# RWKV's triangular inverses on four quarters of the TensorE array, and a fourth raw weight buffer from the FFN on

## The chip, the cores and the metric

The kernel runs on one core of a Trainium2 chip. The metric is device microseconds (us) of one launch. The kernel before has a median of 892.22 us over three runs (888.31 to 893.76).

## The reference, cut to what matters

Two blocks of a language model run one after the other on 256 tokens of width 1024, in fp32. The first block mixes with RWKV-7 and with retention, merges both through gates, and follows with a convolved FFN (width 2816); the second has a Mamba-2 mixer, a per-layer embedding, sliding-window attention and another embedding. The change touches the inside of RWKV-7 and the loading of weights.

RWKV-7's delta rule is computed in chunks of 64 tokens. For each of 8 heads and each of 4 chunks a 64x64 unit lower triangular matrix must be inverted: 32 inverses.

```python
def first_block(x, positions, ...):
    ...
        y_rw = rwkv7_mixer(p_rw, ...)
        y_ret = retention_mixer(p_ret, positions)
        merged = (jax.nn.sigmoid(g_rw.astype(jnp.float32)) * (y_rw @ w_branch_rw[l])
                  + jax.nn.sigmoid(g_ret.astype(jnp.float32)) * (y_ret @ w_branch_ret[l]))
        h = h + rms_norm(merged @ w_out[l], norm_mix_post[l])
        f = conv_ffn(rms_norm(h, norm_ffn_pre[l]), ffn_w_up[l], ffn_conv_w[l], ffn_conv_b[l], ffn_w_down[l])
        h = h + rms_norm(f, norm_ffn_post[l])
```

## The kernel before, in words

**Weights.** Every large matmul takes its weights from a `Stream` (lines 214 to 247). `next()` takes a raw buffer of 128x1024 fp32 (512 KB) and has SyncE's queue load it (L232). ScalarE rounds it to the high part (`whi`, `lhi`, ... L254) and VectorE subtracts that from the raw values for the low part (L255); L249 and L250 are the same with a gain. A product is three matmuls, high times high, high times low, low times high (L258 to L260). `raw_turn` (L211) names the raw buffers, three of them, taken in turn; a load waits until ScalarE and VectorE are done with what its buffer held. In the last stages a second pool of three is added.

**Inverses.** `product` (L600) makes eight 64x64 fp32 matmuls (L606) into one PSUM bank: four pairs of heads `f`, and for each the two heads `x`. Head x=0 has its rows in partitions 64 to 127, head x=1 in 0 to 63, and each writes the partitions that it reads, so two of the array's four 64x64 quarters work, those on its diagonal. The trace shows two MATMUL records for each of these fp32 matmuls. `inverse(c)` (L611) inverts the eight matrices of chunk c by doubling the size of the blocks in five rounds. A round is a product of the matrix with the transposed estimate `Tm`, a copy of it to SBUF with its sign turned (`Pn`, ScalarE, L621), a product of the estimate `X` with that, a masked copy into `Tm` (VectorE, L626) and a transpose of `Tm` into `X` (VectorE, L627). The last round has no transpose (L630).

**Order.** `rwkv` (L636) runs the inverses of four chunks in step, a half round at a time; after them it walks through the chunks: a right-hand side (L650, L653), a copy `R` (L655), a product with the inverse (L606), copies into `VU` (L658, L659), a new state (L666). Outputs follow for each two chunks (L690, L696), then normalisation, transposes (L716) and gating. `weave` puts a step of this between steps of the other stream: the projections of retention and of the gates, whose large matmuls fill TensorE while RWKV's small steps wait for ScalarE and VectorE. The framework then orders each engine's instructions; each engine works through its own in that order.

**Pools.** `cst` holds all constants, `msk` the masks of the inverses, both for the whole program. Pool `p1` lives through the mixers, and `late_pool` opens after it.

## Time and profile before

| | |
|---|---|
| profiled execution | 891.34 us |
| its span | 889.5 us |
| median of 3 runs | 892.22 us |
| TensorE busy (PE) | 858.5 us, 97% of the span |
| VectorE busy (DVE) | 651.4 us, 73% |
| ScalarE busy (ACT) | 522.6 us, 59% |
| share of 16 DMA engines in SyncE's loads | 48.0% |

PE is TensorE's matmul row, PEld its weight loads, SP is SyncE, whose queue issues the loads. A row of the timeline merges instructions of one group that follow each other: start, time from the first start to the last end, engine, line, and in brackets the idle time of the engine just before and what ended it. In groups, "x16 | 6.3, 421 | 0.1" says sixteen instructions, 6.3 us busy, 421 ns each on average, 0.1 us of idle time before them. Instructions of one engine overlap at their ends, so a mean is longer than the step from one to the next.

### The profile page before, as it was taken

Reading aid. Unit: us, or ns where it says so; the run is one execution under the profiler, and the core shown is the slowest. Engines: PE = TensorE matmul, PEld = TensorE weight load, DVE = VectorE, ACT = ScalarE, POOL = GpSimd, SP = SyncE. Lnnn points to the kernel's source line nnn. Section 1 sums busy time; section 2 is a strip of 40 time slices with the busy share of each in tenths; the row PEclk is TensorE's granted clock in tenths of the full one; section 3 lists DMA queues with packets and bytes.
Section 4 is the critical chain, followed back from the end, with each engine's and each line's share of the span. In section 5 each row is a group of like instructions: output and inputs, shape, how many; then the busy total and the mean of one; then the engine's idle time right before and its main releaser. Section 6 shows DMA issues by size and latency. Waiting matters only on the chain.

```text
span 889.5 us, 15883 instructions
## 1 busy us (share of the span) xinstructions
PE 858.5 (97%) x6226; PEld 749.9 (84%) x6226; DVE 651.4 (73%) x1117; ACT 522.6 (59%) x935; POOL 70.6 (8%) x105
## 2 busy tenths in 40 slices
PE   9999999999999999999999988999999999999997
PEld 6788788789998889989999878988888888878776
DVE  7778865774755778888788878889775569857643
ACT  6555533454544556656656657768776467756652
POOL 2000000100100100000000000001101003402000
PEclk9999999999999999999999999999999999999999
DMA  8443341334566476656555376643534558543311
GB/s 278 145 132 105 131 126 68 103 112 137 179 219 213 156 245 212 217 190 188 191 190 178 104 242 209 222 152 141 189 121 141 165 176 289 165 172 105 117 36 36
DMA packets 42284, 144.44 MB, mean 162 GB/s; under 512 B 5009, under 2 KB 5601, under 8 KB 42210
## 3 DMA queue, kind: packets, MB, share of 16 engines
q1 hardware_dynamic: 41600, 141.32, 48.0%
q0 software_dynamic: 608, 2.11, 0.9%
q8 instruction: 49, 0.80, 0.4%
q14 instruction: 25, 0.20, 0.1%
q10 hardware_dynamic: 2, 0.00, 0.0%
HBM read 140.24 MB, written 3.18 MB: 161 GB/s over the span
## 4 chain that ended last, share of the span: by engine, by line
PE 44%; issue 23%; DVE 14%; DMA 9%; ACT 5%; POOL 3%; ACTq 0%; POOLq 0%; SPq 0%; DVEq 0%
PE mm L258 10%; PE mm L260 10%; PE mm L259 10%; DVE wlo L255 3%; PE sm L606 3%; DMA raw<-in_w_up 3%; DMA raw<-in_w_br 2%; DMA raw<-in_w_down 2%; ACT whi L254 1%; PE sm L260 1%; PE sm L258 1%; PE sm L259 1%; DVE llo L255 1%; PE sm L285 1%; PE sm L1559 1%
## 5 line engine op out<-in xcount | busy, mean ns | idle before, releaser
L254 ACT ACTIVATE whi<-raw 128x1024 fp32r<-128x1024 f32 (+1 forms) x125 | 128.1, 1028 | 111.0 <-PE mm L259 35.2
L255 DVE TENSOR_TENSOR wlo<-raw,whi 128x1024 fp32r<-128x1024 f32 (+1 forms) x124 | 147.2, 1191 | 58.8 <-ACT whi L254 57.4
L260 PE MATMUL mm<-xTh,wlo 128*128 128x256 f32 x616 | 173.7, 282 | 2.8 <-DVE wlo L255 2.8
L258 PE MATMUL mm<-xTh,whi 128*128 128x256 f32 x616 | 174.9, 284 | 0.2 <-ACT xTh L254 0.2
L259 PE MATMUL mm<-xTl,whi 128*128 128x256 f32 x616 | 173.4, 282 | 0.3 <-DVE xTl L255 0.3
L260 PEld LDWEIGHTS mm<-xTh,wlo 128*128 128x128 f32 x616 | 116.2, 189 | 3.9 <-DVE wlo L255 3.5
L258 PEld LDWEIGHTS mm<-xTh,whi 128*128 128x128 f32 x616 | 116.3, 189 | 2.6 <-issue 0.7
L259 PEld LDWEIGHTS mm<-xTl,whi 128*128 128x128 f32 x616 | 116.4, 189 | 2.1 <-DVE xTl L255 0.5
L258 PE MATMUL mm<-whi,xTh 128*128 128x512 f32 x168 | 68.3, 407 | 0.0
L260 PE MATMUL mm<-whi,xTl 128*128 128x512 f32 x168 | 67.3, 401 | 0.0
L259 PE MATMUL mm<-wlo,xTh 128*128 128x512 f32 x168 | 66.0, 394 | 0.0
L258 PE MATMUL mm<-lhi,xTh 128*128 128x512 f32 (+1 forms) x156 | 61.1, 393 | 0.5 <-ACT xTh L254 0.5
L260 PE MATMUL mm<-lhi,xTl 128*128 128x512 f32 (+1 forms) x156 | 60.1, 386 | 0.5 <-DVE xTl L255 0.5
L259 PE MATMUL mm<-llo,xTh 128*128 128x512 f32 (+1 forms) x156 | 60.3, 386 | 0.0
L255 DVE TENSOR_TENSOR llo<-raw,lhi 128x1024 fp32r<-128x1024 f32 x38 | 47.0, 1239 | 11.8 <-ACT lhi L254 11.7
L254 ACT ACTIVATE lhi<-raw 128x1024 fp32r<-128x1024 f32 x38 | 40.0, 1057 | 19.2 <-DMA raw<-in_w_down 12.8
L1010 DVE SCALAR_TENSOR_TENSOR fc<-mm,par,fc 128x255 f32<-128x255 f32 x88 | 42.1, 478 | 8.9 <-ACT fc L1007 8.2
L259 PE MATMUL mm<-xTl,ehi 128*128 128x256 f32 x168 | 47.3, 281 | 0.0
L260 PE MATMUL mm<-xTh,elo 128*128 128x256 f32 x168 | 47.3, 281 | 0.0
L258 PE MATMUL mm<-xTh,ehi 128*128 128x256 f32 x168 | 47.2, 281 | 0.0
L1007 ACT ACTIVATE fc<-mm,par 128x256 f32<-128x256 f32 x44 | 24.4, 554 | 23.8 <-DVE fc L1010 23.8
L255 DVE TENSOR_TENSOR elo<-raw,ehi 128x1024 fp32r<-128x1024 f32 (+1 forms) x27 | 31.8, 1183 | 8.6 <-ACT ehi L254 8.2
(485 smaller groups left out, 2029.3 us busy)
## 6 DMA issues: line engine op xcount, KB each, us to landing
raw<-in_w_up SPq DMA_DIRECT2D x44, 512.0 KB, 4.0
raw<-in_w_xbc SPq DMA_DIRECT2D x25, 512.0 KB, 4.2
raw<-in_w_ret SPq DMA_DIRECT2D x24, 512.0 KB, 3.9
raw<-in_w_down SPq DMA_DIRECT2D x22, 512.0 KB, 4.4
raw<-in_w_gate SPq DMA_DIRECT2D x16, 512.0 KB, 3.6
raw<-in_w_z SPq DMA_DIRECT2D x16, 512.0 KB, 4.0
raw<-in_w_so SPq DMA_DIRECT2D x16, 512.0 KB, 3.8
raw<-in_w_pg SPq DMA_DIRECT2D x16, 512.0 KB, 4.5
```

What stands on the lines that cost most here:

```text
L254: first = S.activation(out=hi, in_=src, func=AF.Copy)
L255: last_split[:] = first.ins, (eng or V).tensor_tensor(out=lo, in0=src, in1=hi.bitcast(F32), op=sub).ins
L258: PE.matmul(out, sh, mh, start=start, stop=False)
L259: PE.matmul(out, sh, ml, start=False, stop=False)
L260: return PE.matmul(out, sl, mh, start=False, stop=stop).ins
L285: last = PE.transpose(ps[:, i, :], src[:, (j + i) * P:(j + i + 1) * P], ident)
L606: PE.matmul(fv(px)[u, f, :], lhsT(f, x), rhs[u, f, :], start=True, stop=True)
L1007: S.activation(out=c, in_=ps, func=AF.Identity, scale=wv[:, (ntap - 1) * nf + i:(ntap - 1) * nf + i + 1], bias=bv[:, i:i + 1])
L1010: V.scalar_tensor_tensor(out=c[:, d:], in0=ps[:, :T - d], scalar=wv[:, j:j + 1], in1=c[:, d:], op0=mult, op1=add)
L1559: PE.matmul(po[:, o:o + 64], eT[:, j * P:(j + 1) * P], vn[kb][:, kv * 64:(kv + 1) * 64], start=(kb == 0), stop=(kb == nk - 1))
```

## The change

Two chunks are now inverted together, by `inverse(p)` for a pair p of chunks. The sixteen heads-by-chunks are dealt to four quarters: s says whether heads 0 to 3 or 4 to 7, x the head as before, k counts the four matrices of one quarter. `product` takes two banks, one for each s, and its loop visits four different quarters one after the other. For s=1 the first product writes the other half of the partitions than it reads (`home`), and the estimate `X` of s=1 lies in that other half, so it is transposed by two instructions of 64 partitions (L637) where s=0 needs one (L634). The walk through the chunks deals its matmuls in the same way and splits `R` and `VU` by s.

The constants are split: those that only the mixers use (`cst1`) and the masks go into pool `p1`. In the room that this frees, `late_pool` holds a fourth raw buffer, `rawl`, which from the FFN on takes its turn after the three others; in the last stages there are seven where there were six. The tables of angles share a `u` buffer.

```diff
 CONST, N_CONST = _layout([
-    ("ident", 128), ("ones2", 128), ("heads2", 2), ("gmask", 128), ("tri", 128), ("amask", 256),
-    ("fdec", 8), ("qdec", 8), ("qd2", 8), ("rdec", 4), ("scan64", 256), ("scan128", 256),
+    ("ident", 128), ("amask", 256), ("scan128", 256),
+    ("ones2", 128), ("heads2", 2), ("gmask", 128), ("tri", 128),
+    ("fdec", 8), ("qdec", 8), ("qd2", 8), ("rdec", 4), ("scan64", 256),
     ("ifreq", 32), ("xinit", 64), ("eye64", 64),
 ])
+N_ALL = CONST["ones2"][0]
...
-    nc.sync.dma_start(out=cst[:, P:], in_=io["cst"][:, P:])
+    nc.sync.dma_start(out=cst1, in_=io["cst"][:, N_ALL:])
+    nc.sync.dma_start(out=cst[:, P:], in_=io["cst"][:, P:N_ALL])
...
-    def product(lhsT, rhs):
-        px = sm()
-        for f in range(4):
+    def home(s, x):
+        return UH[x] if s == 0 else VH[x]
+
+    def product(lhsT, rhs, out):
+        banks = [fv(sm()), fv(sm())]
+        for k in range(4):
+            for s in range(2):
+                for x in range(2):
+                    PE.matmul(banks[s][out(s, x), k, :], lhsT(s, x, k), rhs(s, x, k), start=True, stop=True)
+        return banks
...
-    def inverse(c):
+    def inverse(p):
...
+        def turned(s):
+            if s == 0:
+                V.transpose(out=X[s], in_=Tm[s])
+            else:
+                for x in range(2):
+                    V.transpose(out=X[s][VH[x]], in_=Tm[s][UH[x]])
...
         for i in range(1, 6):
-            pp = product(lambda f, x: Gm[UH[x], c, 2 * f + x, 0:64], Tm)
-            Pn = tl(p1, [P, 4, 64], "Pn", 3)
-            S.activation(out=Pn, in_=pp, func=AF.Copy, scale=-1.0)
+            pp = product(lambda s, x, k: Gm[UH[x], 2 * p + k // 2, 4 * s + 2 * (k % 2) + x, 0:64],
+                         lambda s, x, k: Tm[s][UH[x], k, :], home)
+            Pn = []
+            for s in range(2):
+                Pn.append(tl(p1, [P, 4, 64], "Pn", 4))
+                S.activation(out=Pn[s], in_=pp[s], func=AF.Copy, scale=-1.0)
             yield
             if i < 5:
-                pq = product(lambda f, x: X[UH[x], f, :], Pn)
-                V.copy_predicated(out=Tm, mask=half4(f"m{i}", msk, MASKI), data=pq)
-                V.transpose(out=X, in_=Tm)
+                pq = product(lambda s, x, k: X[s][home(s, x), k, :], lambda s, x, k: Pn[s][home(s, x), k, :],
+                             lambda s, x: UH[x])
+                for s in range(2):
+                    V.copy_predicated(out=Tm[s], mask=mask(f"m{i}"), data=pq[s])
+                    turned(s)
...
-        gens = [inverse(c) for c in range(4)]
+        gens = [inverse(p) for p in range(2)]
...
-            pr = sm()
+            pr = [fv(sm()), fv(sm())]
             R = tl(p1, [P, 4, 64], "R", 1)
-            S.activation(out=R, in_=fv(pr), func=AF.Copy)
+            places = [(f, s, x) for f in range(2) for s in range(2) for x in range(2)]
...
+            for s in range(2):
+                S.activation(out=R[:, 2 * s:2 * s + 2, :], in_=pr[s][:, 0:2, :], func=AF.Copy)
             yield
-            pu = product(lambda f, x: X_c[c][UH[x], f, :], R)
+            pu = [fv(sm()), fv(sm())]
+            for f, s, x in places:
+                PE.matmul(pu[s][UH[x], f, :], X_c[c // 2][s][home(s, x), 2 * (c % 2) + f, :], R[home(s, x), 2 * s + f, :],
+                          start=True, stop=True)
...
     late_pool = pool("late")
     wtags["l"] = (late_pool, 4)
+    raw_turn[:] = [(wp, "raw", 3)] * 3 + [(late_pool, "rawl", 1)]
...
-    raw_turn.append((p4, "raw4", 3))
+    raw_turn[:] = [(wp, "raw", 3), (p4, "raw4", 3)] * 3 + [(late_pool, "rawl", 1)]
```

On TensorE, between the second product of the first round (`sm<-Pn,u`) and the first product of the second (`sm<-u,Gm`), there stood in the kernel before six large matmuls of retention:

```order
L606 MATMUL sm_1339<-Pn_1298,u_1284 64x64 x8
L258 MATMUL mm_1060<-whi_1352,xTh_79 128x512
L259 MATMUL mm_1060<-wlo_1353,xTh_79 128x512
L260 MATMUL mm_1060<-whi_1352,xTl_80 128x512
L258 MATMUL mm_1060<-whi_1352,xTh_79 128x512
L259 MATMUL mm_1060<-wlo_1353,xTh_79 128x512
L260 MATMUL mm_1060<-whi_1352,xTl_80 128x512
L606 MATMUL sm_1362<-u_1236,Gm_262 64x64 x8
```

In the changed kernel the same place reads so; `sm_1330` and `sm_1331` are the banks of s=0 and s=1 of the second pair of chunks, `sm_1365` and `sm_1366` those of the first pair in the next round:

```order
L619 MATMUL sm_1331<-Pn_1299,u_1272 64x64 x2
L619 MATMUL sm_1330<-Pn_1297,u_1267 64x64 x2
L619 MATMUL sm_1331<-Pn_1299,u_1272 64x64 x2
L619 MATMUL sm_1365<-u_1233,Gm_259 64x64 x2
L619 MATMUL sm_1366<-u_1238,Gm_259 64x64 x2
```

Two matmuls of a bank now alternate with two of the other, where eight of one bank stood together, and no large matmul is left between the two products at this one place; at the other changes of product 6 to 12 large ones, or retention's smaller ones, stand between them as before.

On VectorE, the masked copies and transposes after the second product of the first round, up to the next low part of a weight (`wlo`), were in the kernel before:

```order
L255 TENSOR_TENSOR wlo<-raw,whi 128x1024 x2
L626 COPY_PREDICATED u<-msk,sm 128x256 x2
L627 STREAM_TRANSPOSE u<-u 128x256 x2
L626 COPY_PREDICATED u<-msk,sm 128x256 x2
L627 STREAM_TRANSPOSE u<-u 128x256 x2
L255 TENSOR_TENSOR wlo<-raw,whi 128x1024
```

In the changed kernel, with the last two transposes of the setting up (L637) ahead of them:

```order
L256 TENSOR_TENSOR wlo<-raw,whi 128x1024
L637 STREAM_TRANSPOSE u<-u 64x256 x2
L663 COPY_PREDICATED u<-msk,sm 128x256 x2
L634 STREAM_TRANSPOSE u<-u 128x256
L637 STREAM_TRANSPOSE u<-u 64x256 x2
L663 COPY_PREDICATED u<-msk,sm 128x256 x2
L634 STREAM_TRANSPOSE u<-u 128x256
L637 STREAM_TRANSPOSE u<-u 64x256 x2
L256 TENSOR_TENSOR wlo<-raw,whi 128x1024
```

Eight instructions of a round have become ten.

On SyncE's queue in the middle of the FFN, the loads of the up and down weights were in the kernel before:

```order
L232 DMA raw<-in_w_down 128x1024
L232 DMA raw<-in_w_up 128x1024 x2
L232 DMA raw<-in_w_down 128x1024
L232 DMA raw<-in_w_up 128x1024 x2
L232 DMA raw<-in_w_down 128x1024
```

In the changed kernel every fourth goes to `rawl`:

```order
L233 DMA raw<-in_w_down 128x1024
L233 DMA rawl<-in_w_up 128x1024
L233 DMA raw<-in_w_up 128x1024 x3
L233 DMA rawl<-in_w_down 128x1024
L233 DMA raw<-in_w_up 128x1024
L233 DMA rawl<-in_w_up 128x1024
```

A load can now be issued one buffer earlier, and the three of a step of the FFN no longer always stand in the order down, up, up.

## Rows read from the trace of the kernel before

**Rows 1.** Page, busy time of each engine and chain that ended last.

```profile
PE 858.5 (97%) x6226; PEld 749.9 (84%) x6226; DVE 651.4 (73%) x1117; ACT 522.6 (59%) x935; POOL 70.6 (8%) x105
...
PE 44%; issue 23%; DVE 14%; DMA 9%; ACT 5%; POOL 3%; ACTq 0%; POOLq 0%; SPq 0%; DVEq 0%
```

**Rows 2.** Stretches: length, busy PE, PEld, DVE, ACT, POOL, granted clock, DMA share, GB/s.

```profile
109.00:115.78 6.78, 6.78 (x140) 5.62 (x139) 6.23 (x12) 2.68 (x6) 0.00 (x0) 1.00 0.42 131
115.78:149.00 33.22, 33.22 (x616) 28.44 (x615) 19.05 (x40) 13.16 (x25) 0.00 (x0) 1.00 0.32 103
...
325.00:500.00 175.00, 172.67 (x1219) 160.48 (x1218) 144.40 (x239) 109.28 (x177) 0.00 (x0) 1.00 0.58 186
```

**Rows 3.** Timeline of TensorE, products of the inverses on two quarters.

```profile
111.71 0.68 PE L606 MATMUL sm<-u,Gm 64*64 64x64 f32 x16
...
115.78 2.08 PE L606 MATMUL sm<-u,Gm 64*64 64x64 f32 x64
117.79 0.50 PE L258 MATMUL mm<-whi,xTh 128*128 128x512 f32 x1
118.13 0.40 PE L259 MATMUL mm<-wlo,xTh 128*128 128x512 f32 x1
118.36 0.39 PE L260 MATMUL mm<-whi,xTl 128*128 128x512 f32 x1
```

**Rows 4.** Timeline of TensorE, outputs of the last two chunks.

```profile
218.24 0.69 PE L690 MATMUL sm<-St,KR 64*64 64x64 f32 x32
```

**Rows 5.** Groups of VectorE, 109 to 149 us.

```profile
L255 DVE TENSOR_TENSOR wlo<-raw,whi 128x1024 fp32r<-128x1024 f32 x8 | 9.7, 1214 | 6.6 <-ACT whi L254 6.6
L627 DVE STREAM_TRANSPOSE u<-u 128x256 f32<-128x256 f32 x16 | 6.3, 421 | 0.1
L626 DVE COPY_PREDICATED u<-msk,sm 128x256 f32<-128x256 uint8 x16 | 6.2, 425 | 6.5 <-PE sm L606 6.5
```

**Rows 6.** Timeline of VectorE, one round, and its next wait.

```profile
114.05 0.77 DVE L626 COPY_PREDICATED u<-msk,sm 128x256 f32<-128x256 uint8 x2
114.71 0.76 DVE L627 STREAM_TRANSPOSE u<-u 128x256 f32<-128x256 f32 x2
115.40 0.74 DVE L626 COPY_PREDICATED u<-msk,sm 128x256 f32<-128x256 uint8 x2
116.04 0.75 DVE L627 STREAM_TRANSPOSE u<-u 128x256 f32<-128x256 f32 x2
121.06 1.22 DVE L255 TENSOR_TENSOR wlo<-raw,whi 128x1024 fp32r<-128x1024 f32 x1 [4.27 <-ACT whi L254]
```

**Rows 7.** Groups of the walk through the chunks, 149 to 225 us.

```profile
L653 PE MATMUL sm<-VU,Gm 64*64 64x64 f32 x64 | 3.6, 220 | 0.0
L650 PE MATMUL sm<-St,KR 64*64 64x64 f32 x48 | 3.1, 224 | 0.0
...
L606 PE MATMUL sm<-R,u 64*64 64x64 f32 x64 | 2.7, 224 | 0.0
```

**Rows 8.** Timeline of TensorE, transposes that it waited for.

```profile
30.87 0.44 PE L476 MATMUL sm<-cst,u 128*128 128x128 f32 x2 [0.62 <-ACT u L469]
...
190.94 0.63 PE L716 MATMUL sm<-cst,u 128*128 128x128 f32 x4 [0.79 <-DVE u L712]
```

**Rows 9.** Waits, 325 to 500 us (the FFN): total, times, longest.

```profile
ACT lhi L254 <- DMA raw<-in_w_down: 12.8, 13, 1.8
...
ACT ehi L254 <- DMA raw<-in_w_up: 8.3, 5, 2.4
ACT whi L254 <- DMA raw<-in_w_up: 7.4, 7, 1.9
```

**Rows 10.** Timeline in the FFN, ScalarE and TensorE.

```profile
383.25 1.06 ACT L254 ACTIVATE lhi<-raw 128x1024 fp32r<-128x1024 f32 x1 [1.75 <-DMA raw<-in_w_down]
...
385.61 0.50 PE L258 MATMUL sm<-lhi,fah 128*128 128x512 f32 x1 [1.14 <-ACT fah L254]
...
387.09 0.50 PE L260 MATMUL sm<-lhi,fal 128*128 128x512 f32 x1 [0.75 <-DVE fal L255]
```

**Rows 11.** Timeline of TensorE in the Mamba projections.

```profile
543.62 0.38 PE L260 MATMUL mm<-xTh,wlo 128*128 128x256 f32 x1 [1.77 <-DVE wlo L255]
547.98 0.39 PE L260 MATMUL mm<-xTh,wlo 128*128 128x256 f32 x1 [1.03 <-DVE wlo L255]
```

More of the change, by code (lines that the diff above doesn't have):

```diff
@@ L166, in tile_block @@
     ppd = tl(dp, [4, P, D], "ppd")
-    cst = tl(gp, [P, N_CONST], "cst")
+    cst = tl(gp, [P, N_ALL], "cst")
     h_t = [tl(gp, [P, D], f"h{t}") for t in range(2)]
-    msk = tl(gp, [P, N_MASKI], "msk", dt=U8)
     par = tl(gp, [P, N_PAR], "par")
@@ L176, in C @@
         lo, hi = CONST[name]
-        return cst[:, lo:hi]
+        return cst[:, lo:hi] if hi <= N_ALL else cst1[:, lo - N_ALL:hi - N_ALL]
     def PR(name):
@@ L192, in angles @@
     def angles():
-        posf = tl(p1, [P, 4], "posf")
+        room = u2()
+        ang, n, r = (room[:, i * 128:(i + 1) * 128].rearrange("p (a l) -> p a l", a=4) for i in range(3))
+        posf = room[:, 384:388]
         with tc.issue_after(last_split[1]):
             V.tensor_copy(out=posf, in_=pos)
-        ang = tl(p1, [P, 4, 32], "ang")
         V.tensor_tensor(out=ang, in0=posf.unsqueeze(2).to_broadcast([P, 4, 32]),
@@ L326, in tile_block @@
     p1 = pool("p1", ph)
+    cst1 = tl(p1, [P, N_CONST - N_ALL], "cst1")
+    msk = tl(p1, [P, N_MASKI], "msk", dt=U8)
     def u2(shape=(P, 512)):
@@ L595, in fv, with half4 @@
         return ps[:, 0:256].rearrange("p (f l) -> p f l", f=4)
-    def half4(name, const=cst, off=CONST):
-        lo, hi = off[name]
-        return const[:, lo:hi].unsqueeze(1).to_broadcast([P, 4, 64])
-    def product(lhsT, rhs):
-        px = sm()
-        for f in range(4):
-            for x in range(2):
-                u = UH[x]
-                PE.matmul(fv(px)[u, f, :], lhsT(f, x), rhs[u, f, :], start=True, stop=True)
-        return fv(px)
-    X_c = {}
-    def inverse(c):
-        X, Tm = (a_.rearrange("p (f l) -> p f l", f=4) for a_ in duo())
-        for x in range(2):
-            V.tensor_tensor(out=X[UH[x]], in0=Gm[UH[x], c, x::2, 0:64], in1=half4("xinit")[UH[x]], op=mult)
-        V.tensor_tensor(out=X, in0=X, in1=half4("eye64"), op=add)
-        V.transpose(out=Tm, in_=X)
-        for i in range(1, 6):
-            pp = product(lambda f, x: Gm[UH[x], c, 2 * f + x, 0:64], Tm)
-            Pn = tl(p1, [P, 4, 64], "Pn", 3)
-            S.activation(out=Pn, in_=pp, func=AF.Copy, scale=-1.0)
+    def half4(v):
+        return v.unsqueeze(1).to_broadcast([P, 4, 64])
@@ new lines, in mask, with L @@
+    def mask(name):
+        lo, hi = MASKI[name]
+        return half4(msk[:, lo:hi])
+    def home(s, x):
[7 more added lines that the diff above has]
+        return banks
+    X_c = {}
+    def inverse(p):
+        X, Tm = [], []
+        def L(s, x):
+            return Gm[UH[x], 2 * p:2 * p + 2, 4 * s + x:4 * s + 4:2, 0:64]
+        def turned(s):
[4 more added lines that the diff above has]
+                    V.transpose(out=X[s][VH[x]], in_=Tm[s][UH[x]])
+        xinit = C("xinit").unsqueeze(1).unsqueeze(1).to_broadcast([P, 2, 2, 64])
+        for s in range(2):
+            a, b = (a_.rearrange("p (f l) -> p f l", f=4) for a_ in duo())
+            for x in range(2):
+                V.tensor_tensor(out=a[UH[x]].rearrange("p (c f) l -> p c f l", c=2), in0=L(s, x), in1=xinit[UH[x]], op=mult)
+            V.tensor_tensor(out=a, in0=a, in1=half4(C("eye64")), op=add)
+            V.transpose(out=b, in_=a)
+            X.append(a)
+            Tm.append(b)
+            if s:
+                turned(s)
+        for i in range(1, 6):
+            pp = product(lambda s, x, k: Gm[UH[x], 2 * p + k // 2, 4 * s + 2 * (k % 2) + x, 0:64],
[4 more added lines that the diff above has]
+                S.activation(out=Pn[s], in_=pp[s], func=AF.Copy, scale=-1.0)
@@ L622, in inverse @@
             yield
             if i < 5:
-                pq = product(lambda f, x: X[UH[x], f, :], Pn)
-                V.copy_predicated(out=Tm, mask=half4(f"m{i}", msk, MASKI), data=pq)
-                V.transpose(out=X, in_=Tm)
-            else:
-                px = product(lambda f, x: Pn[UH[x], f, :], X)
-                V.copy_predicated(out=X, mask=half4("t5", msk, MASKI), data=px)
+                pq = product(lambda s, x, k: X[s][home(s, x), k, :], lambda s, x, k: Pn[s][home(s, x), k, :],
+                             lambda s, x: UH[x])
@@ L631, in inverse @@
+                for s in range(2):
+                    V.copy_predicated(out=Tm[s], mask=mask(f"m{i}"), data=pq[s])
+                    turned(s)
+            else:
+                px = product(lambda s, x, k: Pn[s][home(s, x), k, :], lambda s, x, k: X[s][home(s, x), k, :], home)
+                for s in range(2):
+                    V.copy_predicated(out=X[s], mask=mask("t5"), data=px[s])
             yield
-        X_c[c] = X
+        X_c[p] = X
     yrT = (tl(p1, [P, 4, T], "yrTh", 1, F32R), tl(p1, [P, 4, T], "yrTl", 1, F32R))
```

26 lines of the change are left out of this document (14 added, 12 removed).

## The prediction

> **What bounds the kernel now.** I read the page's busy times first: TensorE is busy for 858.5 of 889.5 us, VectorE for 73%, and TensorE leads the chain that ended last with 44% [rows 1]. So a change gains where it shortens TensorE's own work or fills one of the 31 us in which it idles. The stretches come next. From 109 to 149 us, where the inverses lie, TensorE has no idle time at all and runs at a granted clock of 1.00, the level of 2.4 GHz; VectorE is busy for 6.23 + 19.05 = 25.3 of these 40 us, ScalarE for 15.8 [rows 2]. In the FFN TensorE idles for only 175 - 172.67 = 2.3 us, with the DMA engines at a share of 0.58 [rows 2]. The timelines then tell what a product of the inverses costs, and the waits what the loads hold up.
>
> **Four quarters.** A half round of the inverses is 64 records of 64x64 on TensorE and takes 2.08 us; 16 records take 0.68 us [rows 3]. The difference, 1.40 us for 48 records, is 29.2 ns each, and 0.21 us is fixed. There the records use two quarters. The outputs of the last two chunks are the one place where the kernel already visits four quarters in turn: x picks the half of the rows, the chunk's parity the half of the columns. Its 32 records take 0.69 us [rows 4], with the same 0.21 us 15.0 ns each, half of 29.2. So four quarters run at once. A half round would take 0.21 + 64 x 0.015 = 1.17 us, 0.91 less.
>
> There are ten half rounds. In the first one, half of the 64 records still run two by two, because the scheduler took the banks of the second pair apart (24 matmuls, later 8): that one saves some 0.5 us. Together 9 x 0.91 + 0.5 = 8.7 us of TensorE time.
>
> Two rules of the Trainium skill speak against this. The 32 records took 0.69 us from the first start to the last end, and one takes 0.22 us; that leaves 15 ns from start to start [rows 4, 7]. The Trainium skill, "TensorE: Matmul & The Clock Gate" (Back-to-back issue gap), gives an issue floor of about 25 ns; by that the 816 records of the change (640 here, 176 in the walk below) would save an estimated 3.4 us instead of 11.2, and the time would be about 888. The row contradicts it for matmuls in different quarters.
>
> The old product writes one bank from both halves of the rows, and its two quarters overlap, with 29.2 ns a record [rows 3]; the row with four at once has one half of the rows to a bank [rows 4]. The Trainium skill, "TensorEngine Tiling (Array Packing)" (Restrictions and Gotchas), says that different row tiles can't use one PSUM bank at the same time. By that rule the new product, which writes each bank from both halves of the rows, would gain nothing; the old one's overlap speaks against it. As a mechanism it is the second rival below.
>
> **What VectorE puts against it.** A round has eight instructions of VectorE on the path from the second product to the next round: 0.77 + 0.76 + 0.74 + 0.75 us less overlaps, from 114.05 to 116.79, 2.74 us [rows 6], or 0.34 us each. It gets ten, 3.4 us: for each pair of chunks two masked copies, then three transposes, of which two have half the partitions. The rows show no transpose of 64 partitions. By rows 5 one of 128 partitions has a mean of 421 ns; I take the same, since each of them still walks through 256 columns, with half of it as the lower bound. Twelve more in all (eight in the rounds, four in the setting up) are 4.1 us at 0.34, 2 at least. VectorE has 40 - 25.3 = 14.7 us free here, and after the change 40 - 7 - 25.3 - 4.1 = 3.6. It still fits, but tightly.
>
> Where does TensorE wait? The next round's first product for a pair needs that pair's two copies. After the second product of the first pair (0.5 us), its copies end some 0.9 us later, the second pair's 1.7 us after them, as three transposes and two copies stand between. Where 12 large matmuls lie between the products, 12 x 0.23 = 2.8 us by the starts of rows 3, both fit beside them. After the first round none lies there, as the order shows: TensorE has one pair's product (0.5 us) as cover each time, and waits about 0.4 + 1.2 = 1.6 us. The last two transposes of the setting up stand behind low parts of weights of 1.2 us each [rows 5], so the second pair's product is late by 0 to 1.5 us, I take 0.6. Before the last round only retention's short matmuls give cover: 0.3. Sum of new waits 2.5 us; bounds 0, and 7.9 if each of the four returns waits like the first and the setting up costs its 1.5. Queued behind a waiting product are retention's large matmuls, and behind those ScalarE's next high part, which waits for the weight buffers.
>
> The inverses give -8.7 + 2.5 = -6.2 us, between -8.7 and -0.8.
>
> **The walk through the chunks.** L653, L650 and L606 have 64 + 48 + 64 = 176 records [rows 7], all on two quarters now and on four after: 176 x 14.2 ns = -2.5 us. The copies R and VU become two of half the size: four more instructions of VectorE, eight of ScalarE, each under the 0.41 and 0.39 us of a whole one. After each of them the order on TensorE puts 4 to 48 large matmuls or retention's, so I cost them at 0.3 us. That is -2.2 us, between -2.5 and 0 (without that cover, 12 times 0.2).
>
> Two waits of TensorE lose their ground by the new order: L716 at 190.94 (0.79 us) gets, by the order, 45 large matmuls ahead of it instead of 38, and L476 at 30.87 (0.62) 19 instead of 8 [rows 8]. I take -1.0, between -1.4 and 0, the work moved being done at another time.
>
> **The fourth raw buffer.** In the FFN ScalarE waits for loads often: 12.8 + 8.3 + 7.4 us [rows 9]. But TensorE's whole idle time there is 2.3 us, and one event makes most of it: the high part of a down weight waits 1.75 us for its load, what ScalarE does next (`fah`) is late, and TensorE waits 1.14 and then 0.75 us [rows 10]. A load issued one buffer earlier ends this. What is late next is VectorE's queue, which costs TensorE nothing there now. I take -1.9; the bound is -2.3, and 0 if the scheduler's other order makes such an event elsewhere. The Mamba projections lose 1.77 + 1.03 us to VectorE [rows 11], whose order between two low parts stays nearly as long: 0, at best -2.8. The seventh buffer of the last stages: 0, within 1 either way. The constants now come in two loads of the same bytes: 0.
>
> **The sum**, against the profiled execution's 891.3 us: -6.2 - 2.2 - 1.0 - 1.9 = -11.3, so 880.0. The median of the runs shown is 0.9 us above the profiled one: 880.9 us. I forecast 881.
>
> **The rivals.**
> - More than that: VectorE keeps up, the new waits come to 0.5 us, and the other order of the Mamba stage lifts its 2.8 us: -2.0 - 2.8 - 1 = 6 us further, 875. For it: VectorE's copies of 64 partitions may be short. Against: VectorE's free time of 3.6 us.
> - The pairs stay pairs: two quarters at a time, whatever the loop. Then the 11.2 us of TensorE time stay, VectorE's extra work hides beside it, and the raw buffer with the two waits gives -2.9: 889. What overlaps in part lies between that and the forecast. Against: rows 4. For: there the banks are dealt in another way.
> - Slower than before: VectorE's and ScalarE's queues, in order, expose each round. Low parts of weights stand ahead of the masked copies, and they wait for ScalarE's high parts, and those for TensorE to free a weight buffer (4.27 us at 121.06) [rows 6]. If the matmul that frees it stands behind the product, the large matmuls cover nothing, and each of four returns shows its 3.4 us, the setting up its 1.5, the walk 2.4: 17.5 us against 8.7 + 2.5 + 1.0 + 1.9 = 14.1, so 895.6. It decides from some 2.5 us a return on. Against: TensorE is never idle there today, with the same kind of order.
>
> **How the numbers follow.** Forecast 0.60, its own range 876 to 886; more 0.14; pairs, or overlap in part, 0.19; slower than before 0.07. A difference under 1%, 8.9 us, can hardly be told from none here; the bounds are 883.3 and 901.1. Of the forecast's cases 0.50 lie below 883.3, of that rival's 0.03; with the 0.14 that is 0.67 faster. Slower by over 1% takes the last rival at more than its price: 0.03. The rest, 0.30, is within 1%. The range from 872 to 890 leaves out the slower rival, some of the pairs and a little below.
>
> **What would show it.** Right: 64 records of L619 in about 1.2 us; TensorE idle by 2 to 3 us in the inverses, first between the second product of round one and the next; inverses over some 33 us instead of 40; no wait for `fah` of over 1 us in the FFN. Wrong: L619 at 29 ns a record; waits on copies after every round; or idle time in the FFN and later of more than 2 us over before, where the scheduler's new order lies.

## The result, and the profile after

The changed kernel takes 882.19 us (median of four runs, 881.74 to 884.42), beside 892.99 us for the kernel before: a ratio of 0.9899, with a 95% interval of 0.9869 to 0.9929. Run again, six times, it took 883.85 us, 0.9918 [0.9890, 0.9947]. The forecast was 881. The profiled execution took 884.42 us, 6.9 us less than the one of before.

The total came out as forecast, and its parts did not. The page first, busy times and the chain [rows 1]:

```profile
PE 853.1 (97%) x6226; PEld 744.9 (84%) x6226; DVE 657.6 (74%) x1133; ACT 519.8 (59%) x941; POOL 67.5 (8%) x105
...
PE 61%; issue 20%; DVE 10%; ACT 3%; POOL 3%; DMA 2%; ACTq 0%; POOLq 0%; DVEq 0%
```

Next the stretches, with the columns of [rows 2]; the eighth is the granted clock:

```profile
108.95:112.36 3.41, 3.41 (x53) 2.95 (x53) 3.41 (x6) 1.14 (x4) 0.00 (x0) 0.50 0.05 14
112.36:146.07 33.71, 31.87 (x703) 25.73 (x701) 27.08 (x55) 13.85 (x27) 0.00 (x0) 1.00 0.36 120
225.00:228.40 3.40, 3.40 (x18) 3.40 (x17) 2.41 (x6) 1.91 (x5) 0.00 (x0) 0.50 0.51 164
279.60:283.00 3.40, 3.40 (x17) 3.40 (x17) 2.39 (x5) 1.37 (x2) 0.00 (x0) 0.50 0.59 139
317.20:320.60 3.40, 3.40 (x19) 3.40 (x18) 1.60 (x2) 0.11 (x1) 0.00 (x0) 0.50 0.90 257
325.00:500.00 175.00, 175.00 (x1242) 164.15 (x1241) 144.41 (x242) 108.93 (x178) 0.56 (x1) 1.00 0.58 191
```

Two things are to be seen. In this stretch of the FFN TensorE no longer idles: it is busy for 175.00 of 175 us, against 172.67. And four stretches stand at a clock of 0.50, the level of 1.2 GHz, where before had one within the program (515.28 to 518.69 us). The timeline of TensorE answers to [rows 3, 8]:

```profile
107.50 0.52 PE L515 MATMUL sm<-cst,bonus 128*128 128x128 f32 x3 [1.37 <-DVE bonus L416]
...
109.00 1.97 PE L619 MATMUL sm<-u,Gm 64*64 64x64 f32 x48
...
116.58 1.00 PE L619 MATMUL sm<-u,Gm 64*64 64x64 f32 x32
118.62 1.11 PE L619 MATMUL sm<-u,Gm 64*64 64x64 f32 x32 [1.03 <-DVE u L663]
...
122.41 1.16 PE L619 MATMUL sm<-Pn,u 64*64 64x64 f32 x64
123.50 0.50 PE L259 MATMUL mm<-whi,xTh 128*128 128x512 f32 x1
...
139.44 0.69 PE L619 MATMUL sm<-u,Gm 64*64 64x64 f32 x32
140.59 1.01 PE L619 MATMUL sm<-u,Gm 64*64 64x64 f32 x32 [0.46 <-DVE u L663]
...
143.99 2.08 PE L619 MATMUL sm<-u,Pn 64*64 64x64 f32 x64
...
189.44 0.63 PE L763 MATMUL sm<-cst,u 128*128 128x128 f32 x4 [1.68 <-DVE u L759]
```

64 records take 1.16 us, where 1.17 was forecast. But the last half round still takes 2.08, the first 48 records take 1.97 at half clock, and the wait behind the walk's normalisation is 1.68 us instead of 0.79.

### The stages side by side

All kernels run the same count of matmul records in each stage, so lengths can be compared. I measure from the start of the first product of the inverses, of the first matmul behind the last product, of the first high matmul on `ytT`, of the two groups of `xs` transposes (FFN's input and Mamba's), to the start of the last matmul. "Branches" are the products that take the two mixers' outputs, the gates and the merged product, up to the FFN's input; "rest" is all behind the FFN. In brackets: the us of it at a clock of 0.50. All are single profiled executions; the experiments of the other rows are explained below.

| kernel | inverses | walk | branches | FFN | rest |
|---|---|---|---|---|---|
| before | 39.88 | 71.02 | 88.59 | 198.95 | 377.12 (3.4) |
| changed | 37.00 (3.4) | 70.83 | 90.45 (6.8) | 198.62 (3.4) | 372.00 |
| changed, again | 36.94 (3.4) | 70.83 | 90.71 (6.8) | 196.49 | 372.33 |
| quarters alone | 35.81 | 70.83 | 90.92 (3.4) | 199.19 | 379.95 (6.8) |
| buffer alone | 40.03 | 71.05 | 86.87 | 197.88 (3.4) | 372.43 |
| buffer in the FFN's turn only | 40.03 | 71.05 | 87.05 | 198.42 (3.4) | 372.75 |
| all on the diagonal | 39.38 | 72.40 | 90.09 (6.8) | 199.25 (6.8) | 371.72 |
| last half round too | 36.14 (3.4) | 70.84 | 87.85 | 196.49 | 371.88 |

Read by columns: the inverses are 4.1 us shorter at full clock (35.81) and 2.9 with a stretch of half clock in them; the walk is 0.2 us shorter; the FFN is 2.5 us shorter where its clock is undisturbed (196.49 against 198.95); the rest is 4.4 to 5.4 us shorter wherever the buffer is there from the FFN on. The stretches of the rest, first before, then the buffer alone, split this:

```profile
507.49:884.61 377.12, 367.16 (x2164) 311.65 (x2163) 273.49 (x455) 245.79 (x480) 45.02 (x60) 1.00 0.48 159
504.25:876.68 372.43, 365.74 (x2165) 310.69 (x2163) 272.15 (x452) 241.48 (x474) 42.57 (x60) 1.00 0.48 159
```

TensorE idles for 9.96 us there before and for 6.69 with the buffer, 3.3 less. The other 1.4 of the 4.7 us are busy time, and before's 3.4 us at half clock can account for them (half of 3.4 is 1.7).

The branches need a second look. With the buffer alone they are 1.7 us shorter, but TensorE idles as long in them (3.7 us in both). What differs is the step from one large matmul to the next: 18 steps take 2.16 us in the kernel before, and 2.04 in quarters alone, which has no fourth buffer.

```profile
246.99 0.29 PE L258 MATMUL mm<-ytTh,whi 128*128 128x256 f32 x1
...
249.15 0.29 PE L258 MATMUL mm<-yrTh,whi 128*128 128x256 f32 x1
```

```profile
243.06 0.28 PE L259 MATMUL mm<-ytTh,whi 128*128 128x256 f32 x1
...
245.10 0.28 PE L259 MATMUL mm<-yrTh,whi 128*128 128x256 f32 x1
```

All the new kernels step faster on `ytT` and `yrT` (113 to 117 ns on average, against 120), those without the fourth buffer too. So this gain comes without the buffer. What these kernels share is the third part of the change, the constants and masks moved into pool `p1`; no run takes that part alone, so that it is the cause is not shown.

### The profile page after: what moved, and what is told of

Same layout as the page of the kernel before. It is cut to its first block, busy times and chain, and to the rows that moved or that the text cites. A ratio compares the mean times of both kernels' runs of the same rounds, so it can differ in the third digit from the quotient of the medians.

```text
span 882.7 us, 15934 instructions
## 1 busy us (share of the span) xinstructions
PE 853.1 (97%) x6226; PEld 744.9 (84%) x6226; DVE 657.6 (74%) x1133; ACT 519.8 (59%) x941; POOL 67.5 (8%) x105
## 4 chain that ended last, share of the span: by engine, by line
PE 61%; issue 20%; DVE 10%; ACT 3%; POOL 3%; DMA 2%; ACTq 0%; POOLq 0%; DVEq 0%
PE mm L261 14%; PE mm L260 14%; PE mm L259 14%; PE sm L261 3%; PE sm L259 3%; PE sm L260 3%; DVE wlo L256 2%; PE sm L286 2%; DMA raw<-in_w_br 1%; PE sm L1608 1%; PE sm L619 1%; ACT whi L255 1%; PE sm L1289 1%; PE sm L1601 1%; DMA raw<-in_w_gate 1%
## 5 line engine op out<-in xcount | busy, mean ns | idle before, releaser
L255 ACT ACTIVATE whi<-raw 128x1024 fp32r<-128x1024 f32 (+1 forms) x113 | 115.6, 1027 | 105.1 <-PE mm L260 45.0
L256 DVE TENSOR_TENSOR wlo<-raw,whi 128x1024 fp32r<-128x1024 f32 (+1 forms) x112 | 131.8, 1182 | 54.7 <-ACT whi L255 51.0
L256 DVE TENSOR_TENSOR llo<-raw,lhi 128x1024 fp32r<-128x1024 f32 x29 | 35.3, 1221 | 10.0 <-ACT lhi L255 9.7
L261 PEld LDWEIGHTS mm<-whi,xTl 128*128 128x128 f32 x168 | 31.9, 190 | 6.7
L259 PEld LDWEIGHTS mm<-whi,xTh 128*128 128x128 f32 x168 | 31.9, 190 | 6.6 <-issue 0.3
```

What stands on the lines that cost most here:

```text
L255: first = S.activation(out=hi, in_=src, func=AF.Copy)
L256: last_split[:] = first.ins, (eng or V).tensor_tensor(out=lo, in0=src, in1=hi.bitcast(F32), op=sub).ins
L259: PE.matmul(out, sh, mh, start=start, stop=False)
L261: return PE.matmul(out, sl, mh, start=False, stop=stop).ins
```

## The experiments

The theories as they stood are in the texts on record. A is my reading of the two traces side by side, B the prediction's own sum. Every run below keeps the constants and masks where the change put them.

### One part of the change at a time

quarters_only:

```diff
-    raw_turn[:] = [(wp, "raw", 3)] * 3 + [(late_pool, "rawl", 1)]
...
-    raw_turn[:] = [(wp, "raw", 3), (p4, "raw4", 3)] * 3 + [(late_pool, "rawl", 1)]
+    raw_turn.append((p4, "raw4", 3))
```

> The changed kernel without the new raw weight buffer: the FFN streams through three buffers and the Mamba part through six, as in the kernel before; the inverses and the walk stand on four quarters. Theory A (the traces of the two kernels laid side by side): the inverses give about 3 us, the walk nothing that lasts, because a wait for VectorE takes it back, so 3 to 4 us below before (889, ratio 0.996); the FFN shows its stall of about 2.2 us near 385 us again. Theory B (the prediction's own terms): inverses 6.2, walk 2.2, two waits 1.0, together 9.4 us, 883.5 us, ratio 0.9895. Theory C (the clock): the gain in this part is hidden by windows of half clock that the new waits bring, so the time follows the mean granted clock of each run, and a run at the clock of before is 6 us or more below it.

raw_only keeps those lines and takes the inverses and the walk of the kernel before:

```diff
-    def product(lhsT, rhs, out):
-        banks = [fv(sm()), fv(sm())]
...
+    def product(lhsT, rhs):
+        px = sm()
+        for f in range(4):
...
```

> The changed kernel with the inverses, the product helper and the walk of the kernel before (two quarters, three Pn buffers), and with the new raw buffer. Theory A: the FFN's stall of 2.2 us is gone and the Mamba stage gains 3 to 4 us more, because the seventh buffer lets its first weights start earlier: 5 to 7 us below before (887, ratio 0.993). Theory B (the prediction): 1.9 us in the FFN and nothing in Mamba, 891, ratio 0.998. Theory C: the seventh buffer gives nothing and the 500 to 560 us stretch differs only by a half-clock window, so 890.5, with the idle time of TensorE in that stretch still near 6 us.

Quarters alone: 888.28 us beside 891.29, ratio 0.9981 [0.9959, 1.0003]. Buffer alone: 884.15, ratio 0.9927 [0.9903, 0.9950]. So the small term of the prediction carries the change, and the large one is hardly to be told from nothing. B falls on both counts; A named the right order and met the buffer's ratio (0.993), but put the quarters too high (0.996). C falls too: the run of quarters_only at its highest clock, 0.995, took 889.51 us, not 6 us under before. The inverses of quarters_only in the trace, without any half clock:

```profile
109.88:145.76 35.88, 33.78 (x754) 27.39 (x753) 30.32 (x60) 14.84 (x31) 0.00 (x0) 1.00 0.37 114
```

TensorE idles 2.1 us of them, within the 2 to 3 us forecast. What the missing buffer costs is seen in the timeline of the same kernel, the waits of [rows 10, 11] come back:

```profile
383.58 0.50 PE L259 MATMUL sm<-lhi,fah 128*128 128x512 f32 x1 [0.96 <-ACT fah L255]
385.06 0.50 PE L261 MATMUL sm<-lhi,fal 128*128 128x512 f32 x1 [0.74 <-DVE fal L256]
...
544.06 0.39 PE L261 MATMUL mm<-xTh,wlo 128*128 128x256 f32 x1 [1.21 <-DVE wlo L256]
548.42 0.39 PE L261 MATMUL mm<-xTh,wlo 128*128 128x256 f32 x1 [1.03 <-DVE wlo L256]
```

### Which buffer: the fourth of the FFN or the seventh of the last stages

raw_ffn is raw_only with the last stages' turn as before:

```diff
-    raw_turn[:] = [(wp, "raw", 3), (p4, "raw4", 3)] * 3 + [(late_pool, "rawl", 1)]
+    raw_turn[:] = [(wp, "raw", 3), (p4, "raw4", 3)]
```

> The kernel of the run raw_only (inverses and walk of before) with the fourth raw buffer from the FFN on and only the six old ones in the Mamba block's own turn. Theory D (the buffer pays twice: the FFN no longer stalls, and the Mamba projections that are streamed behind the FFN's last weights no longer wait either, while the seventh buffer does little): 884 to 886, ratio about 0.994. Theory E (the seventh buffer carries the Mamba stage's gain): only the FFN's 2.2 us, 888 to 889, ratio 0.9975.

raw_mamba is raw_only without the line of the FFN:

```diff
-    raw_turn[:] = [(wp, "raw", 3)] * 3 + [(late_pool, "rawl", 1)]
```

> The kernel of the run raw_only with three raw buffers through the FFN, and the added one only as the seventh of the Mamba block. Theory D: the FFN stalls near 385 us again (2.2 us), and the waits at the end of the FFN and in the first Mamba projections (0.7, 0.5, 1.4 and 1.2 us) come back: within 1 us of before, ratio 0.9985. Theory E: those waits stay away, 886 to 887, ratio 0.995.

raw_ffn: 886.83 beside 890.62, ratio 0.9948 [0.9925, 0.9970]; its stages are those of raw_only within 0.6 us. Theory D holds: the Mamba projections' waits go with the FFN's buffer. In raw_ffn's timeline, against 1.77 and 1.03 of [rows 11]:

```profile
512.77 1.09 PE L286 MATMUL sm<-cst,xs 128*128 128x128 f32 x8 [1.64 <-DVE xs L962]
...
543.16 0.38 PE L261 MATMUL mm<-xTh,wlo 128*128 128x256 f32 x1 [0.37 <-DVE wlo L256]
```

The waits from 500 to 560 us give a reason: total, times, longest. The kernel before,

```profile
ACT whi L254 <- DMA raw<-in_w_xbc: 4.4, 5, 2.2
DVE wlo L255 <- ACT whi L254: 3.9, 4, 1.7
PE mm L260 <- DVE wlo L255: 2.8, 2, 1.8
```

and raw_ffn:

```profile
ACT whi L255 <- DMA raw<-in_w_xbc: 1.3, 1, 1.3
DVE wlo L256 <- ACT whi L255: 1.1, 2, 1.0
PE mm L261 <- DVE wlo L256: 0.6, 2, 0.4
```

So the loads that ScalarE waited for in this stretch, 4.4 us before, are 1.3 with the buffer, and TensorE's waits for VectorE's low parts shrink with them. The load is not the whole of the chain. Ahead of the longest of these waits, the 1.77 us at 543.62 in the kernel before, stand

```profile
540.55 1.06 ACT L254 ACTIVATE whi<-raw 128x1024 fp32r<-128x1024 f32 x1 [0.76 <-DMA raw<-in_w_xbc]
```

```profile
540.07 1.73 DVE L1128 RECIPROCAL m<-m 32x256 f32<-32x256 f32 x1
...
542.36 1.21 DVE L255 TENSOR_TENSOR wlo<-raw,whi 128x1024 fp32r<-128x1024 f32 x1
```

The high part waited 0.76 us for its load and ended at 541.61; the low part began 0.75 us later, behind other work of VectorE that ran without a break. In raw_ffn the framework also puts VectorE's instructions in another order (the reciprocal stands ahead of another low part). How the 1.77 us divide between load and order is not shown.

raw_mamba: 896.56, slower, 1.0066 [1.0041, 1.0091]. It did not test what it should. SyncE's queue shows it, first in raw_mamba, then in before:

```profile
289.20 1.26 SPq L233 DMA_DIRECT2D raw<-in_w_proj  x2
302.32 0.33 SPq L233 DMA_DIRECT2D rawl<-in_w_pg  x1
302.74 0.38 SPq L233 DMA_DIRECT2D raw<-in_w_up  x1
```

```profile
289.19 1.66 SPq L232 DMA_DIRECT2D raw<-in_w_proj  x2
297.84 2.94 SPq L232 DMA_DIRECT2D raw<-in_w_up  x3
```

The added buffer's first load, for a later stage, stands ahead of the FFN's weights on SyncE's queue, and its room is not free yet. SyncE's waits of raw_mamba, 285 to 320 us:

```profile
SPq L233 <- PE sm L261: 11.8, 1, 11.8
```

It waits 11.8 us for a matmul and is issued at 302.32; the FFN's weights come after it, 4.9 us later than before. TensorE then waits for the FFN's input, 6.04 us where it is 1.07 before (timeline of raw_mamba):

```profile
313.81 1.97 PE L286 MATMUL sm<-cst,xs 128*128 128x128 f32 x8 [6.04 <-DVE xs L961]
```

What the seventh buffer is worth alone stays open; between raw_only and raw_ffn it is 0.3 us in the last stage of the traces and 0.2% in the ratios, less than their intervals.

### Are four quarters what shortens the inverses?

pairs_all puts the loop over s outermost, in `product` and in the walk; pairs_walk in the walk alone:

```diff
-        for k in range(4):
-            for s in range(2):
+        for s in range(2):
+            for k in range(4):
...
-            places = [(f, s, x) for f in range(2) for s in range(2) for x in range(2)]
+            places = [(f, s, x) for s in range(2) for f in range(2) for x in range(2)]
```

> The changed kernel whose products and walk go through one stack after the other (loop over s outermost), so that two quarters work at a time; every instruction on the other engines is the same. Theory A: nine half rounds of 64 records take 2.08 instead of 1.16 us (8.3 us), some 1 to 2 us of it lies under the waits for the set-up and the first return, the walk costs under 1 us: 6 to 8 us over the changed kernel (889, about 4 us below before, ratio 0.996). Theory B (all records are on the path, the walk's too): 8.3 + 2.5 = 10.8 us, the time of before. Theory C (quarters bring little, what was gained came from fewer and wider VectorE and ScalarE operations): under 2 us over the changed kernel, 884.

> The changed kernel with four quarters in the inverses and two at a time in the walk alone. Theory A: the 16-record groups of the walk take 0.68 instead of 0.46 us, and the waits for VectorE behind them shrink by as much: within 0.7 us of the changed kernel (882 to 883, ratio 0.989). Theory B (walk on the path): 2.2 us over the changed kernel, 884.4, ratio 0.9915.

882.36, ratio 0.9903 [0.9878, 0.9929], and 883.76, ratio 0.9917 [0.9891, 0.9942]: both like the changed kernel. But neither undid what it should, as their timelines show, pairs_all in the inverses and pairs_walk in the walk:

```profile
122.45 1.56 PE L619 MATMUL sm<-Pn,u 64*64 64x64 f32 x64
```

```profile
154.47 0.47 PE L694 MATMUL sm<-VU,Gm 64*64 64x64 f32 x16
```

They show 1.56 us instead of 2.08, and 0.47 instead of 0.68: a short block of one stack overlaps with the next stack's. In part pairs_all did undo it: its inverses take 38.71 us, 1.7 more than the changed kernel's 37.00, both with a stretch of half clock. That its time is no longer than the changed kernel's goes with a higher clock (0.997 on average, against 0.993) and with branches of 86.78 us without half clock, against 90.45. So the two times don't decide. diag does it by place: every stack at home in its own half.

```diff
     def home(s, x):
-        return UH[x] if s == 0 else VH[x]
+        return UH[x]
...
         def turned(s):
-            if s == 0:
-                V.transpose(out=X[s], in_=Tm[s])
-            else:
-                for x in range(2):
-                    V.transpose(out=X[s][VH[x]], in_=Tm[s][UH[x]])
+            V.transpose(out=X[s], in_=Tm[s])
...
-            if s:
-                turned(s)
```

> The changed kernel with every stack at home in its own half: the same pairs of chunks, the same tiles and copies, but all products of the inverses use the two diagonal quarters and the walk two at a time, and the second stack's transposes across the halves fall away (twelve transposes of 64 partitions become six of 128, and those of the setting up go). Theory A (four quarters shorten TensorE's path in the inverses): half rounds of 2.08 us, the stretch of the inverses 40 us or more as in the kernel before, against 35.5 to 37 in the changed one; the time lies 2 to 4 us over the changed kernel, near 885, ratio 0.993, unless the clock is higher. Theory G (what TensorE saves there is waited away later, and the mean clock decides): the stretch is longer by 3 to 4 us all the same, but the clock is at 0.997 and the time within 1 us of the changed kernel, ratio 0.990.

> The changed kernel itself, unchanged, so that it stands on the same chip and beside the same runs of before as the run diag, with more runs than the four it had. Theory A and the sum of the parts (quarters alone 0.998, buffer alone 0.993): ratio 0.990 to 0.991, 881 to 883, with a mean granted clock of 0.994. If the parts help each other: ratio below 0.988.

diag: 886.49 beside 891.97, ratio 0.9955 [0.9932, 0.9978]; the changed kernel, beside the same runs of before, 883.85, ratio 0.9918 [0.9890, 0.9947]. diag's inverses, by the stretch and by one half round:

```profile
113.31:152.76 39.45, 39.45 (x754) 33.72 (x753) 24.39 (x49) 15.21 (x31) 0.00 (x0) 1.00 0.33 109
```

```profile
116.45 2.08 PE L619 MATMUL sm<-Pn,u 64*64 64x64 f32 x64
```

From first product to the next matmul it is 39.38 us, 0.5 less than before and 3.6 more than quarters alone, TensorE is never idle in it, and the kernel is 2.6 us over the changed one. So theory A holds for the inverses: the place of the records gives 3.6 of the 4.1 us, the wider tiles 0.5. The intervals of the two ratios overlap, so the size of the whole effect is not sharp.

### Where the rest of the quarters' gain went

In the walk, the 176 records take 4.4 us from start to start where they took 6.3, 1.9 less (forecast 2.5). The large matmuls between them, with the waits that follow them, take 51.3 instead of 49.5, so the walk is shorter by 0.2 us alone.

diag says what takes the saving back. Its walk holds the changed kernel's matmuls in the same order, with the records on the diagonal, where they take 6.4 us. It lasts 72.40 us, 1.6 more than the changed kernel's 70.83: most of the 2.0 us that the records save is still there at the end of the walk. But diag's walk is also 1.4 us longer than the one before (71.02), with records no faster. The constants' new place is not what lengthens it: the buffer alone has that too, and takes 71.05. What is left is the price of dealing the work out anew: the split copies and the order that comes with them. TensorE's longest wait in the walk, 1.68 us in the changed kernel, is as long in diag:

```profile
196.80 0.63 PE L757 MATMUL sm<-cst,u 128*128 128x128 f32 x4 [1.67 <-DVE u L753]
```

So it is not the saved time of the records that comes back in this wait.

Then the clock. I put matmuls into the longest waits, in the changed kernel (after_fill) and in raw_only (raw_fill); their products are overwritten. The gate matmuls of the walk, which are part of the computation, move ahead of the transposes that wait:

```diff
+    def fill(ps, n):
+        for _ in range(n):
+            PE.matmul(ps[:, 0:P], ident, ident, start=True, stop=True)
...
+            if f == 3:
+                fill(pv, 5)
...
-            pt = sm()
-            for f in range(4):
-                PE.transpose(pt[:, f * P:(f + 1) * P], yc[:, 2 * f:2 * f + 2, :].rearrange("p h l -> p (h l)"), ident)
...
             pgt = sm()
             for f in range(4):
                 PE.matmul(pgt[:, f * P:(f + 1) * P], g2w[:, f * P:(f + 1) * P], gd[:, tk], start=True, stop=True)
+            pt = sm()
+            fill(pt, 3)
+            for f in range(4):
+                PE.transpose(pt[:, f * P:(f + 1) * P], yc[:, 2 * f:2 * f + 2, :].rearrange("p h l -> p (h l)"), ident)
...
-            last = transposes(xs[b], 4, xT, t, 4 * b)
+            last = transposes(xs[b], 4, xT, t, 4 * b, fills=6 if t == b == 0 else 0)
```

> The changed kernel with work put into TensorE's longest waits: the four gate matmuls of the walk go ahead of the transposes that wait for the group norm (both are part of the computation), and 5, 3, 3, 6 and 6 matmuls of the identity, whose results are overwritten, ahead of the transposes of the last value feature, of the walk's two tiles and of the two normed inputs. Theory C (the four quarters' gain is given back in stretches of half clock that follow the waits): the mean granted clock rises to 0.998 or more from 0.991 to 0.996, and the time falls by 3 to 5 us, to 878, ratio 0.985. Theory F (the clock falls in any case, whatever TensorE does in the waits): the clock stays between 0.991 and 0.996; only the gate matmuls that fill two waits count, 1 to 2 us: 881, ratio 0.988.

> The kernel of the run raw_only with the same matmuls in its waits. Theory C (with the waits filled, the four quarters show their worth): 2.5 to 4 us over the run after_fill, 882, ratio 0.989. Theory G (the quarters are worth nothing to the end of the kernel, since what the inverses gain is lost in later waits): within 1 us of the run after_fill.

after_fill: 882.68, ratio 0.9909 [0.9886, 0.9931], its clock 0.996 to 0.998. raw_fill: 890.87, ratio 0.9994 [0.9975, 1.0014], 0.990 to 0.998. Of theory C for the changed kernel the higher clock came true (0.998 in four of six runs), and no time was gained by it: 46 records of 0.11 us from start to start are 5 us, and they didn't fill the waits. In after_fill ten of them run, and the wait for `bonus` is 1.31 us after 1.37:

```profile
104.82 1.28 PE L297 MATMUL sm<-cst 128*128 128x128 f32 x10
...
108.11 0.55 PE L523 MATMUL sm<-cst,bonus 128*128 128x128 f32 x3 [1.31 <-DVE bonus L422]
```

In raw_fill they cost some 6 us over raw_only by the ratios (0.9994 against 0.9927), in after_fill next to nothing over the changed kernel; neither theory foresaw that, and why the same matmuls cost so much more there is not shown. With them the quarters would be worth 8.2 us (890.87 less 882.68), without them 1 to 2.5 (0.9927 against 0.9918 and 0.9899); so the first is no price of the quarters.

### The last half round, and a version with both

In the last product s=0 and s=1 read and write the same two quarters, since each writes its `home`. last4 sends the second stack's result to the other half:

```diff
-                px = product(lambda s, x, k: Pn[s][home(s, x), k, :], lambda s, x, k: X[s][home(s, x), k, :], home)
-                for s in range(2):
-                    V.copy_predicated(out=X[s], mask=mask("t5"), data=px[s])
+                px = product(lambda s, x, k: Pn[s][home(s, x), k, :], lambda s, x, k: X[s][home(s, x), k, :],
+                             lambda s, x: UH[x])
+                V.copy_predicated(out=X[0], mask=mask("t5"), data=px[0])
+                for x in range(2):
+                    V.copy_predicated(out=X[1][VH[x]], mask=mask("t5")[UH[x]], data=px[1][UH[x]])
```

> The changed kernel whose last half round (X against the last P) also uses four quarters: the second stack's output goes to the other half and its masked copy comes back across the halves in two instructions instead of one. The order of TensorE's instructions is the same. If the place of the output decides: 64 records in 1.16 instead of 2.08 us, so 0.9 us less on TensorE; the inverses' stretch 0.9 us shorter, less what the added copy costs (0.2 to 0.4): the time 0 to 1 us under the changed kernel, 882 to 883. If the last half round is slow for another reason (it is the only one whose moving operand is X): 2.08 us as before.

last4_spread adds steps of the other stream to last4:

```diff
             rw_feature(8 + f, vm)
             yield
+            if f == 3:
+                yield
...
+            yield
+            yield
             yield
             pt = sm()
```

> The kernel of the run last4 with two more steps of the woven streams ahead of the transposes behind the group norm, and one ahead of the last value feature's transposes, so that large matmuls fall into TensorE's waits there (1.8 us at 189, 1.2 us behind the first round). Theory A (such waits are the rest of what the quarters gave back): 1.2 us less in the inverses, up to 1.8 us less in the walk, 879 to 881, ratio 0.987. Theory G (a wait filled in one place comes back in the next, as in the runs with matmuls in the waits): within 1 us of last4.

Both ran on a chip where before takes 887.27 us. last4: 880.79, ratio 0.9920 [0.9898, 0.9942]; the half round takes what was expected,

```profile
144.12 1.16 PE L619 MATMUL sm<-u,Pn 64*64 64x64 f32 x64
```

and the inverses 36.14 us with a stretch of half clock, 0.9 less than the changed kernel's 37.00 with one. last4_spread: 878.92, ratio 0.9903 [0.9870, 0.9935]. It can't be told from last4, because its six runs reach from 875.61 to 885.07 us, in the order of their mean clock but for two neighbours: 0.998, 0.998, 0.995, 0.996, 0.989, 0.986. Its profiled run (882.03 us) shows a long stretch at half clock in the walk:

```profile
171.00:174.80 3.80, 2.34 (x26) 1.30 (x25) 3.55 (x5) 1.00 (x3) 0.00 (x0) 1.00 0.42 138
174.80:185.00 10.20, 10.20 (x75) 8.20 (x76) 4.35 (x12) 1.69 (x3) 0.00 (x0) 0.50 0.30 103
185.00:200.00 15.00, 15.00 (x130) 14.44 (x131) 11.30 (x19) 8.73 (x15) 2.01 (x1) 1.00 0.31 105
```

TensorE was busy for 2.34 of the 3.80 us ahead of it. The inverses of that run take 34.77 us, without half clock. Both ratios lie within the intervals of the changed kernel's (0.9899 and 0.9918): no version here is shown to beat the changed one.

## Why the prediction was right in its total, point by point

**Four quarters at once: right.** 64 records took 1.16 us against 1.17, and the rival that pairs stay pairs falls. The Trainium skill's issue floor of about 25 ns ("TensorE: Matmul & The Clock Gate", Back-to-back issue gap) and its rule that different row tiles can't use one PSUM bank at the same time ("TensorEngine Tiling (Array Packing)", Restrictions and Gotchas) do not hold here: the records are 15 ns apart, with both halves of the rows in each bank.

**The inverses: mechanism right, term too big.** Forecast -6.2, measured -4.1 at full clock. TensorE idles 2.1 us there (forecast 2.5), with the waits where they were said to be: in quarters_only 0.52 us after the setting up (forecast 0.6), 1.03 after the first round (1.6) and 0.46 before the last (0.3). So the records saved 4.1 + 2.1 = 6.2 us instead of 8.7, and the step that failed is "ten half rounds ... 9 x 0.91 + 0.5". The tenth stays on two quarters (0.92 us, by last4); the code of the change says so, and I did not read it. Three of the groups of 32, which follow a wait or a split, take 1.00, 1.11 and 1.01 us where one without takes 0.69: 1.05 us more. The last half microsecond I can't place. VectorE's part was near: 30.3 us busy instead of 25.3, 5.0 more where 4.1 were forecast; a transpose of 64 partitions takes 440 ns, one of 128 takes 435, as was assumed.

**The walk: failed.** -2.2 forecast, -0.2 measured. The quarters' own part was too high but there: 1.6 us at the end of the walk (72.40 in diag against 70.83) instead of 2.5. The step that failed is "so I cost them at 0.3 us": the split copies, with the order that comes with them, cost 1.4 us (72.40 in diag against 71.02 before).

**The two waits: failed.** -1.0 forecast. L716's wait grew from 0.79 to 1.68 us, which is 0.9 of the walk's 1.4; counting seven more large matmuls ahead of it did not tell when VectorE would be done. L480 no longer waits at 30.9 us, yet the first product starts at 109.00 against 109.03, and the wait for `bonus` ahead of it is 1.37 us where it was 0.78.

**The fourth raw buffer: failed, in the other direction.** -1.9 was forecast. raw_only measured about 0.7% or 6.5 us, of which the 1.7 us of the branches come without the buffer; that leaves some 4.8. In the FFN the term was nearly right (2.5 against the bound of 2.3). The step that failed is "VectorE, whose order between two low parts stays nearly as long: 0, at best -2.8". TensorE idles 3.3 us less behind the FFN: the low parts had been late in part because ScalarE's high parts waited for their loads, 4.4 us in the Mamba stretch, and VectorE's order did not stay the old one.

**The sum: right by two errors that cancel, which is luck.** -9.4 for the quarters with the two waits was 4.3 at best, -1.9 for the buffer was less than half of it, and the faster step of the branches was no term at all.

**What was not in the sum: the clock.** The mean clock of the runs is 0.996 for before (the 22 beside the first four experiments), 0.997 for raw_only, 0.993 for quarters_only and for the changed kernel (ten runs). A stretch of half clock goes with 1.2 us in the inverses (37.00 against 35.81) and 1.4 to 2.1 in the FFN (197.88 and 198.62 against 196.49). A line of one slope through each kernel's own runs (the 114 of before, of the changed kernel and of the first eight experiments) gives 0.6 us for 0.001 of mean clock, with much scatter (it explains 37%). By that estimate the quarters would be worth about 4 us at the clock of raw_only, near the 4.1 + 0.2 of the stages; the two medians behind it (884.15 and 882.19) were not taken side by side. That the quarters cause the lower clock is not shown: pairs_all, which keeps part of the overlap, runs at 0.997, and raw_ffn, which has none, at 0.994.

## What to carry to other kernels

Price a faster piece of TensorE's work together with what its new layout adds. In the inverses the records saved 6.2 us and waits for VectorE took 2.1 back; in the walk the quarters saved 1.6 us and the split copies with their order cost 1.4. When a matmul waits for VectorE, follow the wait back to the load behind it before calling it a matter of VectorE's order alone: one buffer more may be worth more than the change beside it. And test the parts one by one even where the total agrees, since two wrong terms can make a right sum; a part that rides along in every run, as the constants' new place does here, stays unpriced.

## What the runs showed of the hardware

- Which quarters follow each other decides, not only how many are named: 64 records took 2.08 us on the two diagonal quarters, 1.56 where blocks of eight matmuls alternate between two pairs of quarters (pairs_all), 1.16 with four in turn.
- Executions of one kernel on one chip lay up to 9.5 us apart with the mean clock (last4_spread, 875.61 at 0.998 and 885.07 at 0.986). In the changed kernel a wait of 1.37 us at 107.50 was followed by half clock from 108.95 on; one of 1.35 us in quarters_only, at 108.37, was not.
- A load whose room was not free yet (11.8 us of wait in raw_mamba) held up the loads behind it on SyncE's queue: 4.9 us at 298 us, and 6.04 us of idle TensorE behind it.
- The same large matmuls (128x256 on `ytT` and `yrT`, at a granted clock of 1.00) stepped at 120 ns in the branches of the kernel before and at 113 to 117 in all the others, with or without the fourth buffer.
